# Mixture-of-experts layer of a float32 encoder: four conditional places per expert instead of six, and the two token comparisons nested the other way round

## The chip, the cores and the metric

The kernel runs on one core of a Trainium2 chip. The metric is the device time of one execution in microseconds (us); the figure of a kernel is the median of its runs. Rows of the profile call the engines PE (TensorE, matmuls), PEld (its weight loads), DVE (VectorE), ACT (ScalarE), POOL (GpSimd) and SP (SyncE, which issues most DMAs). An L and a number is a line of the kernel, as printed below.

## The reference, cut to what matters

Two layers of an encoder for 512 tokens of width 1024, all in float32. The change touches only the feed-forward part of the second layer, where each token goes to two of eight experts:

```python
logits = hf @ w_router + b_router            # (512, 8)
top_logit, top_idx = lax.top_k(logits, 2)
gate = softmax(top_logit)
# the rows of each expert are gathered, and for every expert e
y = (silu(x_e @ w1[e]) * (x_e @ w3[e])) @ w2[e]      # w1, w3: 1024 x 1408, w2: 1408 x 1024
# and each token gets the sum of its two rows, times their gates
```

How many tokens an expert gets depends on the data; 1024 picks over eight experts make 128 on average.

## The kernel before

The experts are worked through one after the other. Each expert's weights come as 35 **pieces** of 128 rows, numbered by `SEQ`: 0 to 7 and 8 to 15 are the first two 512-wide thirds of w1 and w3 (`u0`, `u1`), 16 to 19 the rows of w2 for the first third (`d0`), 20 to 27 the last, 384-wide third of w1 and w3 (`u2`), 28 to 31 and 32 to 34 the rest of w2 (`d1`, `d2`). A piece is 512 KB, those of `u2` 384 KB.

A piece is fetched by a DMA of SP (L1289) into one of 18 buffers `raw` (two of them are called `wraw`). Then ACT copies it to a rounded high part `whi` (L1304) and DVE subtracts that to get the low part `wlo` (L1306): this is `cut`, and it runs four pieces ahead of the matmuls in a ring of five pairs. Expert e has two sets of rows:

- **A**, its first 128 tokens: `A(j)` multiplies piece j in three passes (high by high, high by low, low by high) with two matmuls each (L1353); the first pass reads `whi`, the second `wlo`.
- **B**, tokens 129 to 192, if there are any: `B(lo, hi, before)` multiplies pieces lo to hi-1 in one pass straight from `raw` (L1357), for 32 more rows or for 64. It stands inside conditions on `cv[e]`, the number of tokens. Such a spot is called a **place** here. `before` names a third whose result is first transposed by PE into the bank `pub` (`turn`, L1393) and copied by ACT to `gB` (L1398); the `u` pieces of B add up in the same bank `pub`, the `d` pieces in another, `pdb`.

Since B reads `raw`, a buffer is free only when B is through with its piece, or when the place has been passed. So `refill` stands at the end of `B`: it fetches piece n + 18 once B has done piece n. After the place `B(8, 16)` that is pieces 26 to 33, after `B(16, 20)` 34 and the next expert's 0 to 2.

PE, ACT and DVE run in the order of the code (a manual schedule); the order of SP's queue is set by the framework. Every engine meets the conditions; one that skips a place still counts up its semaphore there, and for PE that waits until its own matmuls have ended. SP has work inside a condition only where `yb`, the 64 rows' result, is written out (L1411).

The order of one expert before, with `ahead` true for expert 6 alone:

```python
A(*range(8))
B(0, 8)
A(8, 9, 10, 11); turn(0, 128); A(12, 13, 14, 15)
B(8, 16, 0)
A(16, 17, 18); turn(1, 128); A(19)
B(16, 20, 1)
A(*range(20, 28))
B(20, 28)
A(28); half_T(e + 1, 0); A(29); half_T(e + 1, 1); A(30); turn(2, 128); A(31)
B(28, 35 if ahead else 32, 2)
A(32, 33, 34)
if not ahead: B(32, 35)
```

Behind the last expert `merge` splits the results `pd` (of A) and `pdb` (of B) into high and low parts (L163) and spreads them over the tokens with matmuls (L1436).

Of the kernel before, what the change touches and what calls it, by code (L numbers as in the profile page):

```python
# [25 lines left out]
NK = 8  # L26
# [3 lines left out]
NE = 8  # L30
# [14 lines left out]
def trunk(ctx, tc, I, out, dbg=None):  # L45
# [1053 lines left out]
    def moe(j, l, N, nxt):  # L1099
# [104 lines left out]
        def token_ids(es, b, ps, whole=True, make=True, count=True):  # L1204
            c = slice(b * 128, (b + 1) * 128)
            for e in es:
                oh_e = ohs[(2 * e + b) % 3]
                if make:
                    for t in range(NT):
                        ts(oh_e[:, t, :], iota256[:, c], posm[:, t, e:e + 1], None, op0=OP.is_equal)  # L1210
                for t in range(NT if count else 0):
                    done = mm(ps[:, (b * NE + e) * 2:(b * NE + e) * 2 + 2], oh_e[:, t, :], tk2[:, t, :],
                              start=(t == 0), stop=(t == NT - 1))
            if count:
                tm.append(done)
            if whole:
                return numbers(es, b, ps)

        def numbers(es, b, ps):
            q = slice(es[0], es[-1] + 1)  # L1220
            nc.vector.tensor_reduce(out=tif[:, b, q], in_=ps[:, 16 * b:16 * b + 16].rearrange("p (e c) -> p e c", c=2)[:, q],
                                    axis=AX.X, op=OP.add)
            return nc.vector.tensor_copy(TI[:, b, q], tif[:, b, q])

        def gather(xg, idx, src=hd):
            return nc.gpsimd.indirect_dma_start(out=xg, out_offset=None, in_=src,  # L1226
                                         in_offset=bass.IndirectOffsetOnAxis(ap=idx, axis=0))
# [30 lines left out]
        SEQ = []  # L1258
# [32 lines left out]
        def fetch_any(n, er=None):  # L1291
            if n < NW:
                fetch(n, er, nc.sync if er is None else nc.gpsimd)
            else:
                nc.sync.dma_start(out=raws[n % NRAW].rearrange("p (a b) -> p a b", a=2), in_=tail[n - NW])
# [12 lines left out]
        def rows_T(xg, he, banks):  # L1308
            n = xg.shape[0]
            per = 512 // n  # L1310
            for h in range(NK // per):
                for k in range(per):
                    done = nc.tensor.transpose(banks[h][:, k * n:(k + 1) * n],
                                        xg[:, (per * h + k) * 128:(per * h + k + 1) * 128], ident[0:n, 0:n])
                p3 = banks[h].rearrange("p (k q) -> p k q", k=per)
                if n == 128:
                    split(p3, he[0][:, per * h:per * h + per, :], he[1][:, per * h:per * h + per, :])
                else:
                    act(he, p3, AF.Copy)
            return done  # L1320
# [8 lines left out]
        def quads(m, i):  # L1329
            return m == 32  # L1330
# [33 lines left out]
        def evac(i, m):  # L1364
            fw = FCH[i][1]
            if m == 128:
                src, gated = (tA[1] if i == 2 else tA[i])[:, :fw], tA[i % 2][:, :fw]
                act(src, pa_[2 * (i % 2)][:, :fw], AF.Silu)
                (ordered if i == 2 else partial(tt, op=OP.mult))(out=gated, in0=src, in1=pa_[2 * (i % 2) + 1][:, :fw])
            else:  # L1370
                n, w_ = (64, fw // 2) if quads(m, i) else (m, fw)
                act(tB[i % 2][64:64 + n, :w_], pub[0:n, :w_], AF.Silu)
                f = ordered if i == 2 and m == 64 else partial(tt, op=OP.mult)
                f(out=tB[i % 2][0:n, :w_], in0=tB[i % 2][64:64 + n, :w_], in1=pub[64:64 + n, :w_])
# [38 lines left out]
        def fold(m):  # L1413
            gather((xa, ye)[m % 2], G.slot[:, m % 2, m // 2:m // 2 + 1], yd)

        def add(m):
            t, i = m // 2, m % 2
            stt(X[t], (xa, ye)[i], G.gate[i][:, t:t + 1], X[t], op0=OP.mult, op1=OP.add)
# [21 lines left out]
        def expert(e, he, hb=None, total=NW + len(tail), base=None, er=None):  # L1440
            base = e * NP if base is None else base
            last = er is None and e == NE - 1
            state = {"a": 0, "b": 0, "cut": 0, "got": 0}

            def refill():
                while state["got"] < state["b" if er is None else "a"]:
                    n = base + state["got"] + NRAW
                    if n < total:
                        fetch_any(n, er)
                    state["got"] += 1  # L1450

            def hook(j):
                if e > 0 or er is not None:
                    return
                if j == 6:
                    rows_T(xb, heB[0], (pub,))
                    gather(xb, TI[0:64, 1, 1:2])
                if 3 <= j < 15:
                    i = j - 1
                    token_ids([i // 2 + 1], i % 2, (pd[0], pdb)[i % 2], whole=False, make=False)  # L1460
                if 2 <= j < 14:
                    token_ids([j // 2 + 1], j % 2, None, whole=False, count=False)
                if j == 14:
                    for b in range(2):
                        numbers(range(2, NE), b, (pd[0], pdb)[b])

            def A(*js):
                for j in js:
                    m = j // 2 - 8
                    if last and j % 2 == 0 and 0 <= m < 2 * NT:  # L1470
                        fold(m)
                    piece(base + j, 0, he)
                    hook(j)
                    state["a"] = j + 1
                    n = base + j + AHEAD
                    if n < total:
                        cut(n)
                        if er is None and 0 < e < 4:
                            next(rest, None)
                    if last and j % 2 and 0 < m <= 2 * NT:  # L1480
                        add(m - 1)
                    if SEQ[j][0] == "u" and SEQ[j][2] == NK - 1:
                        evac(SEQ[j][1], 128)
                    if er is not None:
                        refill()

            def B(lo, hi, before=None):
                if er is not None:
                    return

                def rest_of(m):
                    if before is not None:
                        turn(before, m)
                    for j in range(lo, hi):
                        piece(base + j, 1, hb, m)
                    if SEQ[hi - 1][0] == "u":
                        evac(SEQ[hi - 1][1], m)
                    if hi == NP and not last:
                        put(yd[NE * 128 + e * 64:NE * 128 + e * 64 + 64, :], m, nc.sync)

                if last:
                    with tc.If(cv[e] > 128):
                        rest_of(64)
                else:
                    with tc.If(cv[e] > 160) as c:
                        rest_of(64)
                    with c.Else():
                        with tc.If(cv[e] > 128):  # L1508
                            rest_of(32)
                state["b"] = hi  # L1510
                refill()

            A(*range(8))
            B(0, 8)
            A(8, 9, 10, 11)
            turn(0, 128)
            A(12, 13, 14, 15)
            B(8, 16, 0)
            A(16, 17, 18)
            turn(1, 128)  # L1520
            A(19)
            B(16, 20, 1)
            A(*range(20, 28))
            B(20, 28)
            A(28)
            if er is None:
                half_T(e + 1, 0)
            A(29)
            if er is None:
                half_T(e + 1, 1)  # L1530
            A(30)
            turn(2, 128)
            if er is None and e + 1 < NE:
                rows_T(xb, heB[(e + 1) % 2], (pa_[2],))
            A(31)
            ahead = er is None and e == NE - 2
            B(28, 35 if ahead else 32, 2)
            A(32, 33, 34)
            if er is None and not last:
                put(yd[e * 128:(e + 1) * 128, :], 128, nc.sync)  # L1540
            if not ahead:
                B(32, 35)
            if last:
                merge()

# [28 lines left out]
        cv = [nc.values_load(iei[:, e:e + 1], min_val=0, max_val=S) for e in range(NE)]  # L1574
# [351 lines left out]
```

## Time and profile before

| | |
|---|---|
| median of 3 runs | 1956.09 us (1955.92 to 1959.73) |
| profiled execution | 1956.71 us, its span 1955.2 us |
| PE busy | 1903.8 us, 97% of the span |
| DVE, ACT, POOL busy | 1186.8, 908.1, 332.7 us |
| DMA in the whole span | 309.39 MB, mean 158 GB/s |

The profiled execution is one of the program's; the span is what the trace covers. Busy time is summed over stages with different limits, so a change in one stage is read from the rows of that stage: the experts run from about 1388 us to 1890 us of the span. A time in a row of a timeline is the start of a group of like instructions, and the next number is how long the group was busy. Matmuls overlap, so the distance of two starts tells what a matmul takes of PE's time.

### The profile page before, as it was taken

The page shows a single profiled execution, that of the slowest core. Times are in us where ns is not written, and L with a number is a line of the kernel's source. Part 1 is how long each engine was busy: PE and PEld are TensorE (multiplying, and loading weights), DVE is VectorE, ACT ScalarE, POOL GpSimd, SP SyncE. Part 2 cuts the span into 40 slices and gives each one's busy share as a digit, 9 for nine tenths or more (in the row PEclk, how much of TensorE's full clock was granted, in tenths as well). Part 3 has the DMA queues.
Part 4 walks back from the last instruction along what each step waited for, and adds up shares of the span by engine and source line. Part 5 has one row for each costly group of instructions (what it writes and reads, how often), then busy time and mean ns, then how long its engine had stood idle before and what let it go on. Part 6 is the DMA issues. An engine that isn't in the chain of part 4 may idle for free. (4 is left out here: it accounts for less than half of the span.)

```text
span 1955.2 us, 27356 instructions
## 1 busy us (share of the span) xinstructions
PE 1903.8 (97%) x9954; PEld 1511.0 (77%) x9954; DVE 1186.8 (61%) x1859; ACT 908.1 (46%) x1349; POOL 332.7 (17%) x632
## 2 busy tenths in 40 slices
PE   7999999999999999999999999999999999999998
PEld 7787777888888888888787677887678877667666
DVE  5867565754333333345767565745899987666674
ACT  5535434333322222254534435333678876556553
POOL 2058220220000000001048320321100000000021
PEclk9999999999999999999999999999999999999999
DMA  5432223234433333432433232335699997756852
GB/s 168 120 116 87 77 91 128 84 95 168 137 97 94 101 97 97 119 91 62 135 114 98 66 92 85 126 96 212 236 370 368 371 357 272 264 202 251 326 160 99
DMA packets 95141, 309.39 MB, mean 158 GB/s; under 512 B 12609, under 2 KB 15681, under 8 KB 94978
## 3 DMA queue, kind: packets, MB, share of 16 engines
q1 hardware_dynamic: 89554, 290.06, 43.5%
q0 software_dynamic: 5280, 16.91, 2.5%
q8 instruction: 100, 1.64, 0.3%
q14 instruction: 63, 0.52, 0.1%
q10 hardware_dynamic: 144, 0.26, 0.0%
HBM read 283.59 MB, written 23.60 MB: 157 GB/s over the span
## 5 line engine op out<-in xcount | busy, mean ns | idle before, releaser
L137 ACT ACTIVATE whi<-wraw 128x1024 fp32r<-128x1024 f32 (+2 forms) x211 | 217.6, 1034 | 483.7 <-PE a L158 265.1
L139 DVE TENSOR_TENSOR wlo<-wraw,whi 128x1024 fp32r<-128x1024 f32 (+2 forms) x211 | 260.0, 1237 | 265.2 <-ACT whi L137 262.9
L157 PE MATMUL a<-hT_hi,whi 128*128 128x512 f32 (+3 forms) x1056 | 412.3, 391 | 1.4 <-ACT hT_hi L163 0.7
L158 PE MATMUL a<-hT_lo,whi 128*128 128x512 f32 (+3 forms) x1056 | 411.5, 390 | 0.8 <-DVE hT_lo L163 0.7
L159 PE MATMUL a<-hT_hi,wlo 128*128 128x512 f32 (+3 forms) x1056 | 411.6, 390 | 0.6 <-DVE wlo L139 0.6
L1306 DVE TENSOR_TENSOR wlo<-raw,whi 128x1024 fp32r<-128x1024 f32 (+1 forms) x198 | 227.8, 1159 | 45.1 <-ACT whi L1304 31.7
L158 PEld LDWEIGHTS a<-hT_lo,whi 128*128 128x128 f32 (+1 forms) x1056 | 197.1, 187 | 42.9 <-issue 2.8
L159 PEld LDWEIGHTS a<-hT_hi,wlo 128*128 128x128 f32 (+1 forms) x1056 | 197.1, 187 | 42.1 <-issue 3.2
L157 PEld LDWEIGHTS a<-hT_hi,whi 128*128 128x128 f32 (+1 forms) x1056 | 196.7, 187 | 42.5 <-issue 1.6
L1304 ACT ACTIVATE whi<-raw 128x1024 fp32r<-128x1024 f32 (+1 forms) x198 | 198.8, 1009 | 48.1 <-PE a L1353 30.4
L157 PE MATMUL a<-whi,hT_hi 128*128 128x256 f32 (+2 forms) x328 | 110.0, 335 | 1.1 <-ACT hT_hi L163 1.1
L159 PE MATMUL a<-whi,hT_lo 128*128 128x256 f32 (+2 forms) x328 | 109.0, 333 | 0.3
L158 PE MATMUL a<-wlo,hT_hi 128*128 128x256 f32 (+2 forms) x328 | 108.6, 331 | 0.0
L664 POOL TENSOR_TENSOR A<-A,t 128x512 f32<-128x512 f32 x48 | 76.4, 1625 | 179.2 <-DVE t L663 179.2
L1353 PE MATMUL a<-whi,heA_hi 128*128 128x512 f32 (+1 forms) x304 | 91.6, 382 | 4.7 <-PEq L1508 1.8
L1353 PE MATMUL a<-wlo,heA_hi 128*128 128x512 f32 (+1 forms) x304 | 88.7, 373 | 0.0
L1353 PE MATMUL a<-whi,heA_lo 128*128 128x512 f32 (+1 forms) x304 | 88.6, 372 | 0.0
L1353 PEld LDWEIGHTS a<-whi,heA_hi 128*128 128x128 f32 x304 | 54.2, 188 | 22.0 <-issue 8.3
L173 POOL TENSOR_SCALAR rs<-ss 128x1 f32<-128x1 f32 x8 | 2.3, 283 | 393.1 <-ACT sq L1773 392.7
L157 PEld LDWEIGHTS a<-whi,hT_hi 128*128 128x128 f32 x328 | 62.5, 191 | 7.0 <-ACT hT_hi L163 1.6
L159 PEld LDWEIGHTS a<-whi,hT_lo 128*128 128x128 f32 x328 | 62.5, 191 | 5.9 <-DVE hT_lo L163 0.9
L1226 POOL DMA_INDIRECT xa<-hd,TI x8 | 12.4, 1553 | 319.0 <-PE a L1326 310.8
(532 smaller groups left out, 3622.5 us busy)
## 6 DMA issues: line engine op xcount, KB each, us to landing
raw<-in_moe_w13a SPq DMA_DIRECT2D x113, 512.0 KB, 7.5
raw<-in_moe_w SPq DMA_DIRECT2D x74, 512.0 KB, 7.9
wraw<-in_w_gate SPq DMA_DIRECT2D x64, 512.0 KB, 3.6
wraw<-in_ffn_w SPq DMA_DIRECT2D x64, 512.0 KB, 3.6
raw<-in_moe_w13b SPq DMA_DIRECT2D x61, 384.0 KB, 7.2
wraw<-in_w_in_T SPq DMA_DIRECT2D x20, 512.0 KB, 3.3
wraw<-in_w_branch SPq DMA_DIRECT2D x16, 512.0 KB, 3.6
wraw<-in_w_o SPq DMA_DIRECT2D x16, 512.0 KB, 3.6
```

Source lines behind the costliest of these rows:

```text
L137: act(hi[:, :n], raw[:, :n], AF.Copy)
L139: tt(out=lo[:, :n], in0=raw[:, :n], in1=hi[:, :n].bitcast(F), op=OP.subtract)
L157: mm(o, a[0], b[0], start=start, stop=False)
L158: mm(o, a[0], b[1], start=False, stop=False)
L159: mm(o, a[1], b[0], start=False, stop=stop)
L173: gts(out=r[:, :n], in0=ss, scalar1=1.0 / dim, scalar2=EPS, op0=OP.mult, op1=OP.add)
L664: gtt(out=A[m], in0=A[m], in1=g[m], op=OP.add)
L1226: return nc.gpsimd.indirect_dma_start(out=xg, out_offset=None, in_=src, in_offset=bass.IndirectOffsetOnAxis(ap=idx, axis=0))
L1304: act(hi[:, :w], raw[:, :w], AF.Copy)
L1306: return tt(out=lo[:, :w], in0=raw[:, :w], in1=hi[:, :w].bitcast(F), op=OP.subtract)
L1353: mm(dst[x][:, :w_], st[sa][:, k, :], w[:, cs[x]], start=first and q == 0, stop=last and q == 2)
```

## The change

The six places become four. `B(8, 16, 0)` and `B(16, 20, 1)` become `B(8, 20, 0)` behind `A(19)`; the transposes of the second third (`before` = 1) move to `B(20, 28, 1)`; `B(28, 32, 2)` and `B(32, 35)` become `B(28, 35, 2)` behind `A(31)` for every expert. The condition "over 128" is now asked first, with "over 160" inside it. Inside `B`, a third's result is evacuated as soon as its last piece is done, since a place may now go on past it.

```diff
                     for j in range(lo, hi):
                         piece(base + j, 1, hb, m)
-                    if SEQ[hi - 1][0] == "u":
-                        evac(SEQ[hi - 1][1], m)
+                        if SEQ[j][0] == "u" and SEQ[j][2] == NK - 1:
+                            evac(SEQ[j][1], m)
...
                 else:
-                    with tc.If(cv[e] > 160) as c:
-                        rest_of(64)
-                    with c.Else():
-                        with tc.If(cv[e] > 128):
+                    with tc.If(cv[e] > 128):
+                        with tc.If(cv[e] > 160) as c:
+                            rest_of(64)
+                        with c.Else():
                             rest_of(32)
...
             turn(0, 128)
-            A(12, 13, 14, 15)
-            B(8, 16, 0)
-            A(16, 17, 18)
+            A(12, 13, 14, 15, 16, 17, 18)
             turn(1, 128)
             A(19)
-            B(16, 20, 1)
+            B(8, 20, 0)
             A(*range(20, 28))
-            B(20, 28)
+            B(20, 28, 1)
...
-            ahead = er is None and e == NE - 2
-            B(28, 35 if ahead else 32, 2)
+            B(28, 35, 2)
             A(32, 33, 34)
...
-            if not ahead:
-                B(32, 35)
```

On PE, the place behind piece 27 of the first expert (L1505 asks "over 128", L1506 "over 160"; `cst`, `ut` are the transposes' operands, `yh` holds B's rows):

```order
 L1505 COMPARE_AND_BRANCH
+L1506 COMPARE_AND_BRANCH
+L1393 MATMUL b<-cst,ut 128x64 x4
 L1357 MATMUL b<-raw_11228,yh 64x384 x2
 L1357 MATMUL b<-raw_11229,yh 64x384 x2
```

The four transposes now stand ahead of the `u2` matmuls, and both write the bank `pub`.

On SP, the first expert's second place; `wraw` and `raw_11660` to `raw_11665` are the buffers of pieces 8 to 15, into which pieces 26 to 33 are fetched:

```order
 L1505 COMPARE_AND_BRANCH
-L1505 UNCONDITIONAL_BRANCH
-L1508 COMPARE_AND_BRANCH
-L1508 UNCONDITIONAL_BRANCH x2
+L1506 COMPARE_AND_BRANCH
+L1506 UNCONDITIONAL_BRANCH x2
+L1505 UNCONDITIONAL_BRANCH
 L1289 DMA wraw<-in_moe_w13b 128x768 x2
 L1289 DMA raw_11660<-in_moe_w 128x1024
 L1289 DMA raw_11661<-in_moe_w 128x1024
 L1289 DMA raw_11662<-in_moe_w 128x1024
```

The fetches stand in the same order behind SP's second place; but that place now ends behind `A(19)`, and before it ended behind `A(15)`.

On PE, the end of the last expert (its conditions are at L1502 in both kernels; `gB_11680` and the buffers after it are pieces 32 to 34 of B, `Sel` belongs to `merge`):

```order
 L1353 MATMUL b<-wlo,gA_hi 128x512 x2
 L1353 MATMUL b<-whi,gA_lo 128x512 x2
-L1502 COMPARE_AND_BRANCH
-L1357 MATMUL b<-raw_11233,gB_11680 64x512 x2
-L1357 MATMUL b<-wraw,gB_11680 64x512 x4
-L1502 UNCONDITIONAL_BRANCH x2
 L1436 MATMUL a<-heA_hi,Sel 128x512
 L1436 MATMUL a<-heA_lo,Sel 128x512
```

The matmuls of B's last three pieces, which stood between the end of A and `merge`, have gone from there (they stand ahead of `A(32)` now).

## Rows read from the trace of the kernel before

**Rows 1.** The page, part 3: DMA queue, kind: packets, MB, share of 16 engines.

```profile
q8 instruction: 100, 1.64, 0.3%
```

**Rows 2.** Windows: experts without B, and with: busy us, PEclk, DMA share, GB/s.

```profile
1450.00:1600.00 150.00, 147.17 (x704) 120.63 (x703) 137.99 (x184) 121.58 (x138) 8.61 (x6) 1.00 0.97 369
1600.00:1890.00 290.00, 286.52 (x1800) 199.08 (x1798) 194.70 (x201) 166.93 (x208) 16.83 (x12) 1.00 0.69 254
```

**Rows 3.** Waits of PE, 1380 to 1900 us: total us, times, longest.

```profile
PE a L1353 <- PEq L1508: 1.8, 5, 1.1
PE b L1357 <- ACT gB L1398: 1.7, 4, 0.5
```

**Rows 4.** The matmuls of L1357 (B): ns min/median/max, first and last start.

```profile
L1357 PE MATMUL b<-raw,yh x532: 326/379/644, 1608.9 to 1872.9; 128*32 128x256 f32 x76, 128*32 128x192 f32 x42, 128*64 128x512 f32 x39, 128*64 128x384 f32 x21
```

**Rows 5.** PE's timeline, expert 1 (no B): skipped places behind pieces 15, 19, 27.

```profile
1467.76 0.62 PE L1353 MATMUL a<-wlo,heA_hi 128*128 128x512 f32 x2
1468.21 0.61 PE L1353 MATMUL a<-whi,heA_lo 128*128 128x512 f32 x2
1468.97 0.70 PE L1353 MATMUL b<-whi,gA_hi 128*128 128x512 f32 x2
1469.52 0.62 PE L1353 MATMUL b<-wlo,gA_hi 128*128 128x512 f32 x2
...
1475.31 0.59 PE L1353 MATMUL a<-whi,heA_hi 128*128 128x384 f32 x2
...
1484.03 0.70 PE L1353 MATMUL b<-whi,gA_hi 128*128 128x512 f32 x2
```

**Rows 6.** PE's timeline, expert 4 (32 rows in B): two places that are taken.

```profile
1608.40 0.61 PE L1353 MATMUL a<-r_hi,heA_lo 128*128 128x512 f32 x2
1608.95 3.66 PE L1357 MATMUL b<-raw,yh 128*32 128x256 f32 x64
1612.54 0.73 PE L1353 MATMUL a<-whi,heA_hi 128*128 128x512 f32 x2
1613.11 0.62 PE L1353 MATMUL a<-wlo,heA_hi 128*128 128x512 f32 x2
...
1634.81 1.93 PE L1357 MATMUL b<-raw,gB 128*32 128x256 f32 x32
1636.67 0.61 PE L1353 MATMUL a<-whi,heA_hi 128*128 128x384 f32 x2
```

**Rows 7.** Windows of 2 us around the second place of expert 1; columns as before.

```profile
1468.00:1470.00 2.00, 1.85 (x9) 1.24 (x8) 2.00 (x5) 1.72 (x3) 0.00 (x0) 1.00 0.11 25
...
1476.00:1478.00 2.00, 2.00 (x14) 2.00 (x13) 1.76 (x5) 1.36 (x3) 0.00 (x0) 1.00 1.02 410
```

**Rows 8.** SP's timeline: expert 1's piece 28 is issued.

```profile
1469.86 0.37 SPq L1289 DMA_DIRECT2D wraw<-in_moe_w  x1
```

**Rows 9.** DMA issues, 1469.8 to 1470.2 us: KB each, us to landing.

```profile
wraw<-in_moe_w SPq DMA_DIRECT2D x1, 512.0 KB, 6.4
```

**Rows 10.** Timelines of ACT and DVE: the cut of one 512 KB piece.

```profile
1467.50 1.06 ACT L1304 ACTIVATE whi<-raw 128x1024 fp32r<-128x1024 f32 x1 [0.30 <-DVE c L1611]
...
1468.61 1.22 DVE L1306 TENSOR_TENSOR wlo<-raw,whi 128x1024 fp32r<-128x1024 f32 x1
```

**Rows 11.** Timelines of PE, ACT and DVE at the end of the last expert.

```profile
1887.05 0.61 PE L1353 MATMUL b<-whi,gA_lo 128*128 128x512 f32 x2
1888.50 1.89 PE L1357 MATMUL b<-wraw,gB 128*64 128x512 f32 x8
1890.32 0.50 PE L1436 MATMUL a<-heA_hi,Sel 128*128 128x512 f32 x1
1892.15 0.40 PE L1436 MATMUL a<-heA_hi,Sel 128*128 128x512 f32 x1
...
1887.48 1.08 ACT L163 ACTIVATE heA_hi<-b 128x512 fp32r<-128x512 f32 x2 [6.08 <-PE b L1353]
...
1888.10 1.29 DVE L163 TENSOR_TENSOR heA_lo<-b,heA_hi 128x512 fp32r<-128x512 f32 x2 [2.44 <-ACT heA_hi L163]
```

## The prediction

> **What bounds the kernel now.** I read the windows first. [...] Without B the DMA engines are busy for 0.97 of the time at 369 GB/s; with B for 0.69. The 704 matmuls of the first window are 2.97 experts (35 pieces x 6, and 27 transposes, make 237 each), so an expert without B lasts 50.5 us, and its DMAs 0.97 x 50.5 = 49.0 us. Below that PE can't bring it, whatever it saves.
>
> The first B matmul starts at 1608.9 us [rows 4]. Experts 0 to 3, the 210 us and more before that, therefore skip every place; 4 to 7 take them, 4 and 6 with 32 rows, 5 and 7 with 64.
>
> Then the places themselves. Two pairs of matmuls stand 0.45 us apart. Across the skipped place behind piece 15 the distance is 0.76, and the pair behind it takes 0.55 [rows 5]: PE empties itself, and fills again. A skipped place costs 0.31 + 0.10, some 0.40 us. Of the 24 such places the list of waits counts only what is above its threshold, 1.8 us [rows 3].
>
> **The change, part by part.**
>
> Skipped places: two fewer in each of experts 0 to 3, 8 x 0.40 = -3.2 us. That the outer comparison is now "over 128" saves a branch on the way past; I cost it at nothing, since the next matmul waits for PE's own last matmul, and the branches lie under that wait. [...]
>
> Taken places: the step into B costs 0.55 - 0.45 = 0.10, the pair behind it 0.57 - 0.45 = 0.12 [rows 6]. 64 matmuls of B and the step out take 3.59 us, 32 take 1.86: so 2 x 1.86 - 3.59 = 0.13 of it is the step out. That is 0.35 us a place. Experts 4, 5 and 7 lose two places, expert 6 one, since it had five: 7 x 0.35 = -2.45 us. In expert 5 (64 rows; expert 7 has one comparison only, as before) a second comparison is now passed at each place; I cost that at nothing, since PE's matmuls of A, already queued, cover the branch.
>
> The transposes of the second third: before, they stood ahead of `d0`, which adds up in `pdb`. Now they stand ahead of `u2`, which adds up in `pub`, the bank that they themselves write. The first `u2` matmul must wait until ACT has copied `pub` to `gB`. That wait is there already at the place behind piece 15, four times, 1.7 us [rows 3]; it stays there and comes a second time: +1.7 us.
>
> The moved fetches: pieces 26 to 33 are issued when the second place is over, and that is now A(20)'s start, not A(16)'s: 1475.31 - 1468.97 = 6.3 us later, less the 0.4 of the place that is gone [rows 5]. Nothing covers this well in experts 0 to 3. At that very moment the DMA engines have run dry: share 0.11 from 1468 to 1470, and 1.02 some microseconds later [rows 7]. What is late next is piece 28, the first of 512 KB. It is issued at 1469.86, 0.89 us behind the place's end, and lands after 6.4 us [rows 8, 9], 7.3 us behind the end. ACT's and DVE's parts of its cut take from 1467.50 to 1469.83, 2.33 us [rows 10], with some 0.1 us of handing over; PE needs the low part only in its second pair, 0.45 us after the start. So A(28) can start 7.3 + 2.0 = 9.3 us behind the end of the second place, and PE comes to it 1484.03 - 1475.31 = 8.7 us behind [rows 5]. The stall is 0.6 us an expert, 2.3 us for four, if the queue is dry each time. It may not be: where the pieces of one expert come 5.9 us later, so do those behind them, and the queue that ran dry about 1468 would then run dry about 1474, just ahead of the new place. Then there is no fresh start and no stall. Bounds 0 and 2.3 us; I take the middle, +1.2 us. In experts 4 to 7, B's own matmuls lie between (3.6 us at the first place alone, rows 6), and with a DMA share of 0.69 I cost the delay at nothing there.
>
> The fetches behind `yb` on SP: SP waits inside the last place for B's result. That place now ends ahead of A(32) to A(34), so the wait ends earlier by three pieces (3 x 3 x 0.45 = 4.1 us), while some fetches that stood ahead of it now stand behind. I cost it at nothing; the cover is the next expert's first pieces, which are in their buffers by then.
>
> The end: B's last three pieces covered the splitting of `pd` before `merge`. The last pair of A starts at 1887.05, its second matmul 0.23 later, at 1887.28. ACT and DVE split two banks from 1887.48 to 1889.39; a third bank, `pdb`, would take half of 1.29 us more on DVE, to about 1890.0, and the fifth matmul of `merge` comes 0.25 later, 3.0 us behind the last matmul of A. Before, it started at 1892.15, and the last of B at 1888.50 + 1.89 - 0.64 (the longest of L1357, rows 4) = 1889.75: 2.4 us [rows 11]. So +0.6 us.
>
> Sum: -3.2 - 2.45 + 1.7 + 1.2 + 0.6 = **-2.15 us**, all of it in the experts. The profiled execution took 1956.71 us and would take 1954.6; the median of the runs is 0.6 us lower, so the forecast in its terms is **1953.9 us**. That is 0.11% less; a difference of under 0.2% (3.9 us) is about what a measurement of this kernel can't tell from no change.
>
> **The rivals.**
>
> *No new stall.* The queue never runs dry at the new place, and `merge` starts as it did: -3.2 - 2.45 + 1.7 = -3.95, 1952.1 us. For it: the DMA cycle of 49.0 us is still under the new 50.5 - 0.8 = 49.7. Against it: only by 0.7 us.
>
> *The switches cost nothing worth saving.* If a merged place drains as long as two did (skipped 0.2, taken 0.1 saved each), the sum is -1.6 - 0.7 + 1.7 + 1.2 + 0.6 = +1.2, 1957.3 us. For it: the rows show the cost of a place, not that of leaving one out. Against it: two drains can hardly lie in one.
>
> *The weights come too late* (slower). The place is experts 0 to 3: the delayed pieces don't catch up, since the DMA engines have 0.7 us an expert to spare, and each piece of the next expert meets PE late as well. Without stalls the sum is -3.35; it is 3.9 us slower from stalls of 7.3 us in all, 1.8 an expert, that is from a landing of piece 28 at 8.5 us behind the place instead of 7.3. With 2.5 us an expert: -3.35 + 10 = +6.7, 1962.8 us. For it: 0.97. Against it: the buffers hold 18 pieces, half an expert, and the next expert's pieces wait in them.
>
> *Longer jumps miss the code.* The place `B(8, 20)` holds half as many more instructions as the longest before, and so does a jump past it; if a skip had to wait for code, that is 1 fetch each: the queue q8 spends 0.3% of 16 x 1955 us on 100 packets, 0.9 us each [rows 1]. Two longer jumps in each of four experts: 8 x 0.9 = +7.2, with the sum +5.1, 1961.1 us. For it: nothing but the size. Against it: 24 skipped places with 1.8 us of counted waits in all [rows 3], so a jump of the present length does not wait for 0.9 us. [...]
>
> **How the numbers follow.** Forecast 0.50; no new stall 0.20; nothing to save 0.17; weights too late 0.08; code 0.05. The range takes in the first three, with 0.5 us for the unlike runs: 1951.6 to 1957.6. Faster by over 0.2% (under 1952.2): half of the second case and 0.05 of the first, 0.15. Slower (over 1960.0): most of the last two, 0.10. Within: 0.75.
>
> **What would show it.** Right: in experts 0 to 3, four distances of about 0.76 between pairs instead of six; one new wait of PE of a few tenths at A(28), ended by a cut that DMA `raw` or `wraw` held up; eight waits for `gB` with 3.4 us; the DMA share in such an expert near 0.98, its dry moment moved to A(20); a wait ahead of L1436 of about 0.6 us more. Wrong: waits of PE for cuts of other pieces than 28, above all of the next expert's; skipped places with over 0.5 us; a pair behind a place that is not 0.10 slower.

## The result, and the profile after

The changed kernel takes **1969.04 us** (median of 7 runs, 1965.72 to 1974.36), the kernel before in the same measurement 1956.61 us (7 runs, 1955.92 to 1959.73): a ratio of 1.0063, interval 1.0053 to 1.0073. It is 0.63% slower, where a loss of over 0.2% had a chance of 0.10. The span of the profiled execution grew from 1955.2 to 1965.8 us, by less than the median; the two longest of the seven runs (1972.45 and 1974.36 us) have the lowest mean granted clock, 0.995, against 0.997 in the profiled one.

First, where. These are the first matmuls of A(0) of expert 0 and of expert 4 in PE's timeline, before and after:

```profile
1387.62 0.62 PE L1353 MATMUL a<-whi,heA_hi 128*128 128x512 f32 x2
1597.88 0.71 PE L1353 MATMUL a<-whi,heA_hi 128*128 128x512 f32 x2
```

```profile
1387.07 0.62 PE L1353 MATMUL a<-whi,heA_hi 128*128 128x512 f32 x2
1602.12 0.62 PE L1353 MATMUL a<-whi,heA_hi 128*128 128x512 f32 x2
```

Experts 0 to 3, where B is skipped, last 215.05 us and lasted 210.26: +4.8, where the sum had -3.2 + 1.2 = -2.0. From expert 4 to the end of the span it is 363.7 us and was 357.3: +6.4, where the sum had -2.45 + 1.7 + 0.6 = -0.15. The stages ahead of the experts give the missing -0.6.

Second, what PE waits for. The list of its waits after the change, 1380 to 1900 us (us in total, times, longest); of before it is [rows 3]:

```profile
PE b L1357 <- ACT gB L1398: 5.3, 7, 2.7
PE a L1313 <- DVE heA_lo L163: 4.9, 4, 1.4
PE b L1357 <- issue: 2.4, 1, 2.4
...
PE b L1353 <- ACT gA_hi L163: 0.5, 1, 0.5
...
PE a L1353 <- ACT whi L1304: 0.4, 1, 0.4
```

The wait for `gB` was 1.7 us; together with the 2.4 us put down to "issue", at the same spot in expert 4, it is now 7.7. The wait of L1313 for `heA_lo` is new. L1313 is the transposing of the next expert's B rows, which stands between A(30) and A(31) in every expert but the last and reuses the bank that `half_T(e + 1, 0)` filled; it can't begin until DVE has read that bank (L163).

Third, why these are late. ACT's waits for weight pieces, 1450 to 1600 us, after the change; before, the list has no wait for a DMA at all:

```profile
ACT whi L1304 <- DMA raw<-in_moe_w: 4.5, 10, 1.8
ACT whi L1304 <- DMA wraw<-in_moe_w: 2.3, 3, 2.0
ACT whi L1304 <- DMA raw<-in_moe_w13b: 2.3, 3, 0.9
```

And the windows after the change: experts without B, and two windows around the end of the new second place of expert 1 (columns as in [rows 2]):

```profile
1450.00:1600.00 150.00, 143.66 (x684) 117.90 (x683) 133.37 (x181) 116.43 (x134) 5.67 (x6) 0.99 0.92 359
1474.00:1475.00 1.00, 0.99 (x5) 0.46 (x3) 0.70 (x2) 0.96 (x2) 0.00 (x0) 1.00 0.00 0
1475.00:1477.00 2.00, 1.86 (x11) 1.89 (x12) 1.78 (x3) 1.37 (x2) 0.00 (x0) 1.00 0.42 104
```

The DMA engines stand still until the place ends, so the queue does run dry at the new place, and their share falls from 0.97 to 0.92. Piece 26 is issued at 1475.11 us, as A(20) starts at 1475.14. The chain from there to PE, in the timelines of ACT, DVE and PE of expert 1:

```profile
1478.20 0.85 ACT L1304 ACTIVATE whi<-raw 128x768 fp32r<-128x768 f32 x1 [0.87 <-DMA raw<-in_moe_w13b]
1479.88 0.85 ACT L1304 ACTIVATE r_hi<-wraw 128x768 fp32r<-128x768 f32 x1 [0.84 <-DMA wraw<-in_moe_w13b]
...
1482.92 1.23 DVE L1306 TENSOR_TENSOR wlo<-wraw,whi 128x1024 fp32r<-128x1024 f32 x1 [1.12 <-ACT whi L1304]
...
1488.76 1.22 DVE L1306 TENSOR_TENSOR r_lo<-raw,r_hi 128x1024 fp32r<-128x1024 f32 x1 [0.21 <-ACT r_hi L1304]
...
1489.97 0.68 DVE L163 TENSOR_TENSOR heA_lo<-a,heA_hi 128x512 fp32r<-128x512 f32 x1
...
1490.71 0.71 PE L1313 MATMUL a<-cst,xb 64*128 64x64 f32 x8 [1.23 <-DVE heA_lo L163]
```

The same rows of DVE before, the cut of piece 28 and the reading of the bank:

```profile
1480.85 1.23 DVE L1306 TENSOR_TENSOR wlo<-wraw,whi 128x1024 fp32r<-128x1024 f32 x1 [0.22 <-ACT whi L1304]
...
1487.84 0.69 DVE L163 TENSOR_TENSOR heA_lo<-a,heA_hi 128x512 fp32r<-128x512 f32 x1
```

DVE read the bank from 1487.84 to 1488.53 before, and PE came to it at 1489.57: 1.0 us to spare. Now it reads it 2.1 us later, though PE is a little earlier, and PE waits for 1.23 us. The delay is there when DVE cuts piece 28 (1482.92 against 1480.85), and from there to the bank the only idle time listed for DVE is the 0.21 us above, so it doesn't shrink. No matmul of A waits for a piece here. What waits stands behind the pieces in the order of ACT and DVE. (The 0.4 us of the list, where A does wait for a cut, are at A(13) of expert 1, at 1464.73 us; ACT had waited 0.88 us for a landing some cuts earlier.)

In experts 4 to 7 it is ACT's copy to `gB`. PE and ACT in expert 6, at the place behind piece 27:

```profile
1796.45 0.33 PE L1393 MATMUL b<-cst,ut 64*128 64x64 f32 x2
1799.47 4.49 PE L1357 MATMUL b<-raw,yh 128*32 128x192 f32 x64 [2.68 <-ACT gB L1398]
...
1796.38 1.06 ACT L1304 ACTIVATE whi<-raw 128x1024 fp32r<-128x1024 f32 x1 [0.19 <-PE a L1353]
1797.81 1.06 ACT L1304 ACTIVATE whi<-raw 128x1024 fp32r<-128x1024 f32 x1 [0.37 <-DMA raw<-in_moe_w]
1798.77 0.47 ACT L1368 ACTIVATE ut<-a 128x384 f32<-128x384 f32 x1
1799.14 0.27 ACT L1398 ACTIVATE gB<-b 128x128 f32<-128x128 f32 x1
```

The transposes are done at 1796.8 (1796.45 + 0.33). ACT copies them at 1799.14, since the cuts of pieces 28 to 31 and the evacuation of A stand ahead of the copy, and those pieces land late. The 64 matmuls behind the wait then take 4.49 us; the same 64 took 2.81 before:

```profile
1791.50 2.81 PE L1357 MATMUL b<-raw,yh 128*32 128x192 f32 x64
```

The windows of the wait and of these matmuls show the granted clock (behind the five busy times): 1.00 while PE is idle, then 0.56:

```profile
1796.80:1799.40 2.60, 0.00 (x0) 0.00 (x0) 2.37 (x3) 2.23 (x4) 0.00 (x0) 1.00 1.03 422
1799.40:1802.40 3.00, 2.93 (x40) 2.03 (x44) 1.34 (x3) 0.01 (x1) 0.00 (x0) 0.56 1.02 419
```

### The profile page after: what moved, and what is told of

The parts are those of the page before. It is cut to its first block, busy times and chain, and to the rows that moved or that the text cites. A ratio compares the mean times of both kernels' runs of the same rounds, so it can differ in the third digit from the quotient of the medians.

```text
span 1965.8 us, 27098 instructions
## 1 busy us (share of the span) xinstructions
PE 1904.0 (97%) x9954; PEld 1515.0 (77%) x9954; DVE 1185.2 (60%) x1859; ACT 905.3 (46%) x1349; POOL 326.3 (17%) x632
## 5 line engine op out<-in xcount | busy, mean ns | idle before, releaser
L158 PEld LDWEIGHTS a<-wlo,hT_hi 128*128 128x128 f32 x328 | 62.7, 191 | 4.7
```

What stands on the lines that cost most here:

```text
L158: mm(o, a[0], b[1], start=False, stop=False)
```

## The experiments

Two causes are to be told apart: the **late fetches** (pieces 26 to 33 issued behind A(19) instead of A(15)), and the **moved transposes** (ahead of `u2`, with ACT's copy behind four cuts). The ends of the experts and the nesting of the comparisons are checked as well. Ratios are to the kernel before, run on the same chip.

**Parts of the change.** `e1_nest`: only the comparisons are nested the other way.

```diff
-                    with tc.If(cv[e] > 160) as c:
-                        rest_of(64)
-                    with c.Else():
-                        with tc.If(cv[e] > 128):
+                    with tc.If(cv[e] > 128):
+                        with tc.If(cv[e] > 160) as c:
+                            rest_of(64)
+                        with c.Else():
```

> Six places as before, only the comparisons are nested the other way round. Fetch theory (the loss of the change comes from pieces 26 to 33, which are issued about 6 us later): no difference, 1956.6 us within 2 us. Nesting theory (the order of the comparisons costs or saves something at each place): 24 skipped places with one comparison fewer, or 64-row places with one more, by up to 0.1 us each, so 1954 or 1959 us, and skipped places whose distance is no longer 0.76 us.

Measured: 0.9998 (0.9989 to 1.0007). The order of the comparisons is worth nothing that can be measured.

`e2_mid`: the middle alone, with the evacuation inside `B` that it needs.

```diff
-            A(12, 13, 14, 15)
-            B(8, 16, 0)
-            A(16, 17, 18)
+            A(12, 13, 14, 15, 16, 17, 18)
             turn(1, 128)
             A(19)
-            B(16, 20, 1)
+            B(8, 20, 0)
             A(*range(20, 28))
-            B(20, 28)
+            B(20, 28, 1)
```

> Only the middle is changed: one place for pieces 8 to 19 behind A(19), and the transposes of the second third ahead of u2. The end of an expert and the comparisons are as before. Fetch theory: the whole loss is here, 1968 to 1971 us, with PE's waits for DVE's heA_lo in experts 0 to 3 (about 4.9 us in all) and for gB in 4 to 7 (over 5 us). Rival (the loss is at the merged last place): under 1960 us.

Measured: 1.0052 (1.0038 to 1.0065), waits for `heA_lo` 5.8 us, for `gB` and "issue" 5.6. The loss is here.

`e3_end`: the end alone.

```diff
-            ahead = er is None and e == NE - 2
-            B(28, 35 if ahead else 32, 2)
+            B(28, 35, 2)
...
-            if not ahead:
-                B(32, 35)
```

> Only the end of an expert is changed: one place for pieces 28 to 34. Fetch theory: four skipped places fewer by 0.31 us, two taken ones by 0.25, and 0.8 us more ahead of the merge of the last expert, so 1955.7 us, no difference that can be measured. Rival (the merged last place is what costs): over 1962 us.

Measured: 0.9996 (0.9987 to 1.0005), as expected.

**Late fetches alone, two misses.** `e4_late`: six places, and only the refill moved.

```diff
-                state["b"] = hi
-                refill()
+                if hi != 16:
+                    state["b"] = hi
+                    refill()
```

> Six places, transposes, and comparisons as before; only the fetches of pieces 26 to 33 are moved from the place behind A(15) to the one behind A(19). Fetch theory: experts 0 to 3 lose 1.5 to 1.9 us each by PE's wait for DVE's heA_lo and its followers, some 6.5 us in all, and 4 to 7 lose nothing since their transposes are where they were: 1963 us. Rival (the moved transposes make the whole loss, and the late fetches are hidden): 1956.6 us within 1 us.

Measured: 1.0002 (0.9993 to 1.0011). It tells nothing about either theory. SP's rows stand in the same order as before, so piece 26 still went out when the place behind A(15) was over (in expert 1 at 1471.34 us, as A(16) starts at 1471.37): here the fetch went out when the place behind the last reader of its buffer was over, not at the spot where the refill is written.

`e9_hold`: eight readers behind A(19), to keep those buffers.

```diff
+            if er is None:
+                for j in range(8, 16):
+                    raw = raws[(base + j) % NRAW]
+                    mm(pdb[0:32, 0:8], raw[:, 0:32], raw[:, 32:40], start=True, stop=True)
             B(16, 20, 1)
```

> Six places, transposes and comparisons as before. Behind A(19), eight added matmuls of 8 columns read the buffers of pieces 8 to 15 once more into a bank that the next d0 overwrites, so that those buffers come free only then, and pieces 26 to 33 are fetched then (the output stays the same). The added matmuls take 0.5 us an expert, 4 us. Late fetches as the cause: PE also waits for DVE's heA_lo in experts 0 to 3 as in the changed kernel, 1.2 to 1.5 us each, 6 us in all, and 10 us more than before. Rival (it is the merged place as such, or what else moved with it): no such wait, and 4 us more than before.

Measured: 1.0304 (1.0290 to 1.0319). A miss again: the refill was still written ahead of the readers, so they read pieces 26 to 33, and PE waited 33.2 us for these to land.

**Taking the causes out one by one.** `e5_tmove`: six places and their fetches as before, the transposes moved.

```diff
-            B(16, 20, 1)
+            B(16, 20)
             A(*range(20, 28))
-            B(20, 28)
+            B(20, 28, 1)
```

> Six places and their fetches as before; only the transposes of the second third of B move from ahead of d0 to ahead of u2. Theory of two causes (late fetches, and ACT's copy to gB that stands behind four cuts): the pieces are in time here, so PE's wait for gB there is 0.9 us in each of experts 4 to 7, as it was in 5 and 7 of the changed kernel, and 3.7 us more than before in all; experts 0 to 3 are unchanged. Rival (the moved transposes alone make the waits of 2.7 us and more): 10 us more than before.

Measured: 1.0009 (1.0000 to 1.0018). The waits of PE:

```profile
PE b L1357 <- ACT gB L1398: 3.0, 7, 0.5
```

With 0.4 us put down to "issue" that is 3.4 us, 1.7 more than before and less than half of the 3.7 expected: with pieces in time, the moved transposes cost just what the prediction gave them. The other 4.3 us of the changed kernel's 7.7 come only with late fetches.

`e6_tin`: the changed kernel with the transposes at the end of the second place.

```diff
                             evac(SEQ[j][1], m)
+                    if lo == 8:
+                        turn(1, m)
...
-            B(20, 28, 1)
+            B(20, 28)
```

> The changed kernel, but the transposes of the second third stand at the end of the place for pieces 8 to 19, behind its d0 matmuls. Two causes: PE's waits for gB ahead of u2 go (9.3 us in the changed kernel), the waits for heA_lo in experts 0 to 3 stay: 2 to 3 us more than before. Rival (what waits for gB would wait for the late pieces anyway, a few matmuls later): 8 us more than before or more.

Measured: 1.0017 (1.0008 to 1.0026). The waits for `gB` are back at those of before, those for `heA_lo` stay:

```profile
PE a L1313 <- DVE heA_lo L163: 5.2, 4, 1.7
...
PE b L1357 <- ACT gB L1398: 1.7, 4, 0.5
```

`e7_early`: the changed kernel with the second place behind A(15).

```diff
-            A(12, 13, 14, 15, 16, 17, 18)
-            turn(1, 128)
-            A(19)
+            A(12, 13, 14, 15)
             B(8, 20, 0)
+            A(16, 17, 18)
+            turn(1, 128)
+            A(19)
```

> The changed kernel with its second place moved up: pieces 8 to 19 of B behind A(15) instead of A(19), so that pieces 26 to 37 are fetched at once when A(15) is over. Two causes: no wait for heA_lo in experts 0 to 3, and 0.9 us for gB in each of 4 to 7: 0.5 us less than before. Rival (it is the size of a place or the number of pieces that a place holds, not its moment, that delays): as slow as the changed kernel, 10 us more than before.

Measured: 1.0000 (0.9991 to 1.0009). There is no wait for `heA_lo`; `gB` as in `e5_tmove`. The same merged place with earlier fetches brings no stall of that kind, so it isn't its size. Most of what the places save is lost again: to `gB`, ahead of the merge, and to 2.9 us in which PE waits for its sequencer behind the new second place (L1505, four times; before, the list has 0.6 us of that kind for these matmuls).

`e8_early_tin`: both edits.

> Both: the second place behind A(15), and the transposes of the second third at its end. Two causes: neither wait is left; twelve places saved at 0.3 us skipped and 0.5 us taken, 0.8 us lost ahead of the merge: 4 us less than before. Rival (a skipped place saves nothing once fetches are on time): no difference.

Measured: 0.9990 (0.9981 to 0.9999), about half of what was expected. (The expectation counts twelve places; in all 15 go.) Neither wait is left, but the one at the second place stays:

```profile
PE b L1353 <- PEq L1507: 3.4, 4, 1.7
```

The skipped place behind A(15) took 1.09 us of PE's idle time in expert 1 and 1.72 in expert 3; PE's own sequencer is named, no weight piece.

**Where the place stands.** The kernel of `e8_early_tin`, transposes at the end of the place, with the place behind A(14), A(16), A(17) and A(18). For A(17) the edit of `e7_early` becomes:

```diff
-            A(12, 13, 14, 15, 16, 17, 18)
+            A(12, 13, 14, 15, 16, 17)
+            B(8, 20, 0)
+            A(18)
             turn(1, 128)
             A(19)
-            B(8, 20, 0)
```

Behind A(14), `e10_at14`:

> As the kernel with the second place behind A(15) and the transposes at its end, but the place behind A(14). In that kernel PE waited 0.9 and 1.6 us at this place in experts 1 and 3, with a packet of the instruction queue in those microseconds. [...] Rival (PE waits there for a weight piece that has not landed): longer here, over 1.6 us an expert, since the place asks for piece 19 earlier.

Measured: 1.0562 (1.0547 to 1.0576), and of no use: there the buffer of piece 19 is refilled with piece 37 before it is cut, so A works with another piece in its place, and ACT waits for that piece to land (41.2 us in two waits from 1450 to 1600 us) with everything that stands behind it.

Behind A(16), `e11_at16`:

> The same with the place behind A(16): pieces 26 to 37 are fetched 1.4 us later than behind A(15). Before, DVE had read heA's bank 1.0 us ahead of PE's next use of it; so late fetches should cost 0 to 0.4 us in each of experts 0 to 3. 3 to 4.6 us less than before without a wait for code, 1 to 2.5 us less with it.

Measured: 0.9978 (0.9968 to 0.9989), no wait for `heA_lo`; PE waits 2.3 us for its sequencer at the place (three times, longest 1.6), which is the wait that the expectation puts down to code.

Behind A(17), `e12_at17`:

> The same with the place behind A(17): fetches 2.8 us later than behind A(15). If the loss grows with the delay beyond a margin of 1.0 us, PE's wait for heA_lo is there again, 0.3 to 1.2 us in each of experts 0 to 3 (it was 0.9 to 1.8 behind A(19)): 1 to 3 us less than before, less a wait for code if one falls here. Rival (the loss comes only when the queue has run dry): no wait for heA_lo, as behind A(15).

Measured: 0.9977 (0.9968 to 0.9986), no wait for `heA_lo` either, 1.4 us at the place. That is 5.2 us less than before (1953.45 against 1958.66), where a margin of 1.0 us would have left 1 to 3. The rival's outcome came, but not for its reason, that the loss comes only when the queue has run dry: the DMA engines stand all but still ahead of this place too, without a loss:

```profile
1470.00:1471.00 1.00, 0.85 (x5) 0.42 (x3) 1.00 (x3) 0.49 (x2) 0.00 (x0) 1.00 0.02 6
```

Behind A(18), `e14_at18`:

> Place for pieces 8 to 19 behind A(18), transposes at its end. Behind A(17) PE never waited for heA_lo, behind A(19) 1.3 us an expert. If the delay costs nothing until a margin of some 4 us is used up and then grows one for one: 0 to 0.6 us an expert here, 3 to 5 us less than before. If it is the moment ahead of the transposes of A that decides: as behind A(19), 3 us more than before.

Measured: 0.9980 (0.9971 to 0.9989). PE has no wait for `heA_lo` at L1313 here, though ACT already waits for landings (11 waits on pieces of `u0` and `u1` alone, 4.8 us from 1450 to 1600 us). In expert 1, piece 26 is issued at 1471.80 us, 1.9 us ahead of A(20) (1473.66); behind A(19) it is issued as A(20) starts, and PE waits 1.1 to 1.4 us an expert. Behind A(18) the late pieces are paid out of the margin, behind A(19) the margin is used up.

**Late fetches alone, done rightly.** `e13_hold2`: the readers of `e9_hold`, and the refill left out at the place behind A(15) as in `e4_late`, so that it stands behind the readers.

> Six places as before. The fetches of pieces 26 to 33 now wait: behind A(19), eight added matmuls of 8 columns read the buffers of pieces 8 to 15 once more (into a bank that the next d0 overwrites; the output stays the same), and the refill stands behind them. The added matmuls take 0.5 to 0.9 us an expert, 4 to 7 us. Late fetches as the cause: PE's wait for DVE's heA_lo appears in experts 0 to 3 with six places too, 0.9 to 1.8 us each, so 8 to 14 us more than before; none in 4 to 7. Rival (it takes the merged place): no wait for heA_lo, 4 to 7 us more than before.

Measured: 1.0057 (1.0044 to 1.0071), 1970.02 against 1958.41 us. PE's waits, with six places:

```profile
PE a L1313 <- DVE heA_lo L163: 3.6, 3, 1.4
```

A(0) of expert 0 starts at 1388.66 us and that of expert 4 at 1607.66: 219.0 us, 8.7 more than before. The readers take 0.6 us an expert (A(20) begins 2.39 us behind A(19), before 1.79), so 6.3 us of it are late fetches. From A(0) of expert 4 to the end of the span it is 1967.7 - 1607.66 = 360.0 us, 2.7 more than before, of which the readers take 2.4: there late fetches alone cost next to nothing. `gB` is at 1.7 us as before. The rival, that it takes the merged place, falls.

**A version that beats both.** `e15_best`: the place behind A(17), transposes at its end (the edit inside `B` is that of `e6_tin`), and in the last expert the two places at the end as before.

```diff
-            A(12, 13, 14, 15, 16, 17, 18)
+            A(12, 13, 14, 15, 16, 17)
+            B(8, 20, 0)
+            A(18)
             turn(1, 128)
             A(19)
-            B(8, 20, 0)
             A(*range(20, 28))
-            B(20, 28, 1)
+            B(20, 28)
...
-            B(28, 35, 2)
+            B(28, 32 if last else 35, 2)
...
             if last:
+                B(32, 35)
                 merge()
```

> Place behind A(17), transposes at its end, and in the last expert alone the two places at the end as before, so that B's last three pieces cover the splitting ahead of the merge again. Merge theory: 0.85 us less than the kernel with the place behind A(17), that is 6 us less than before. Rival (the second place at the end costs as much as it covers): no difference between the two.

Measured: 0.9972 (0.9961 to 0.9983), 1953.32 against 1958.41 us. PE's list has no `heA_lo` of L1313, and `gB` at 1.7 us. The windows show the experts without B near the busy time and DMA share of before [rows 2]:

```profile
1450.00:1600.00 150.00, 147.92 (x714) 122.97 (x713) 138.94 (x187) 122.63 (x139) 8.06 (x6) 1.00 0.96 374
```

Against the kernel behind A(17) the two intervals overlap. In the traces, from A(0) of expert 7 to the end of the span it is 1951.7 - 1808.65 = 143.05 us against 1951.5 - 1807.53 = 143.97: 0.9 us, as the merge theory had it.

## Why the prediction was wrong

**Skipped and taken places: right.** In `e15_best`, which has no new stall, A(0) of expert 0 starts at 1389.75 us and that of expert 4 at 1596.79: 207.04 us, 3.2 less than before, with eight skipped places less. That is the -3.2 of the sum, at 0.40 each: with PE busy for 147.17 of 150 us before [rows 2] and for 147.92 here, what the places took of its time comes off the time. `e3_end` has the same price by itself: from A(0) of expert 0 to that of expert 4 it is 1598.34 - 1389.67 = 208.67 us, 1.6 less for four skipped places. In `e15_best`, from A(0) of expert 4 to that of expert 7, at 1808.65, it takes 211.86 us, and took 1811.69 - 1597.88 = 213.81: 1.95 less for five taken places (two each in 4 and 5, one in 6), 0.39 each instead of 0.35. The rival by which a merged place drains as long as two did is out.

**The moved fetches: this step failed.** The prediction asked when PE needs piece 28, found a stall of 0 to 0.6 us an expert at A(28), and took +1.2 us in all. The mechanism at its start was right: the queue runs dry at the new place (share 0.00 in the window above), and pieces 26 onward land late. PE's need was about right too: the third pair of A(28) starts 1.07, 1.00, 1.25 and 1.22 us behind the first in experts 0 to 3, before 1.00 to 1.01, so A(28) loses 0.5 us in all. What was not followed is what stands behind the cuts on ACT and DVE. Both take it in the order of the code, and DVE is busy for 138 of 150 us [rows 2]; in expert 1 it is 2.1 us late at the cut of piece 28 and still 2.1 us late at `heA_lo`, and ACT's `gA_hi` comes late with it.

With the places saving 3.2 us as above, experts 0 to 3 lost 4.8 + 3.2 = 8.0 us to new stalls, not 1.2. Of these, 4.9 + 0.5 + 0.4 = 5.8 us stand in the list. Some 1.4 us are no wait: in expert 2, behind the wait at L1313, the granted clock was 0.50 from 1543.80 to 1547.10 us (last section). Most of the rest is A(28). Two kernels with the clock at 1.00 in these experts agree: `e13_hold2` has 6.3 us from late fetches alone, and `e6_tin` takes 1602.64 - 1389.42 = 213.22 us for experts 0 to 3, 6.2 more than `e15_best`. The 1.0 us between DVE and PE at L1313 was there to be read in the trace of before. It isn't the whole margin of a fetch: behind A(18) fetches come later than before and PE still doesn't wait.

"In experts 4 to 7 [...] I cost the delay at nothing there" holds for late fetches alone (`e13_hold2`), but not for this change: the cover that was named, B's matmuls and a DMA share of 0.69, covers A. It does not cover ACT, which has four of the late pieces to cut before it copies `gB`, and it is the moved transposes that make PE wait for that copy.

**The moved transposes: the term was right by itself, and wrong beside the late fetches.** +1.7 us was predicted and `e5_tmove` shows 1.7, in the eight waits of 3.4 us that the prediction named; in the changed kernel the waits grew by 6.0 us. To that comes 4.49 - 2.81 = 1.7 us, where the granted clock was 0.50 from 1799.80 to 1803.10 us. With the 2.45 us saved at taken places and the merge, experts 4 to 7 make -2.45 + 6.0 + 1.7 + 0.8 = +6.05, against +6.4 measured.

**The end: right, a little small.** Behind the last matmul of A (its pair starts at 1899.36, and the second 0.23 later) the fifth matmul of L1436 starts at 1902.79, 3.2 us later, where 3.0 was predicted; so +0.8 instead of +0.6. (A slip that changes nothing: by its own words the range ends at 1957.3 + 0.5 = 1957.8, not at 1957.6.)

**The rivals.** The slower one, "the weights come too late", came true in its size (2.0 us an expert, where it asked for 1.8 to be slower by 0.2%), but not in its place: it had each piece of the next expert meet PE late, and the list has 0.4 us of that, at A(13) of expert 1. It had a chance of 0.08 because the buffers were thought to cover PE, and ACT and DVE were not asked. "Longer jumps miss the code" is not what slowed the changed kernel: its list has 1.1 us for PE's sequencer behind skipped places, before it had 2.4 (L1508; [rows 3] shows 1.8 of them, and one wait, at the very first place, was 1.1). But with the place behind A(15) to A(18), PE did wait there, up to 1.7 us. What these waits were for, no run here shows: in `e8_early_tin` the instruction queue has one packet from 1468 to 1470 us, about the wait of 1.09 us, and one from 1567 to 1571, about that of 1.72; but in the kernel before it has one from 1468.0 to 1468.5 and one from 1475 to 1476 us too, within 1 us of two skipped places for which the list has no wait.

## What to carry to other kernels

When a fetch moves, follow it to every engine that touches the data, and on each ask what stands behind it in that engine's order and who waits for that; the margin of the matmul that uses the data is not the margin of the kernel. Two edits that are cheap alone can be dear together, where one makes an engine late and the other puts a wait behind it: in experts 4 to 7 late fetches alone cost some 0.3 us and the moved transposes alone 1.7, and together they made PE wait 6.0 us more and run 1.7 us longer in the 3.3 us with the granted clock at 0.50. Merging two conditional places is worth 0.4 us each here, but the merged place should stand where the buffers come free no later than the margins allow (up to A(18) here), not where the last of its pieces is used.

## What was not expected of the hardware

Twice in the experts the granted clock fell to 0.50 behind a wait of PE. In expert 6 PE had been idle for 2.68 us; the clock was 0.50 from 1799.80 to 1803.10 us, and 64 matmuls took 1.7 us longer (rows above). In expert 2 it had waited for only 1.42 us, at L1313:

```profile
1542.80 0.71 PE L1313 MATMUL a<-cst,xb 64*128 64x64 f32 x8 [1.42 <-DVE heA_lo L163]
1543.43 0.99 PE L1353 MATMUL b<-whi,gA_hi 128*128 128x512 f32 x2
...
1547.22 0.63 PE L1353 MATMUL b<-r_lo,gA_hi 128*128 128x512 f32 x2
```

```profile
1541.00:1543.40 2.40, 0.98 (x12) 0.71 (x10) 2.40 (x3) 2.40 (x5) 0.00 (x0) 1.00 1.02 418
1543.80:1547.10 3.30, 3.15 (x8) 2.07 (x7) 3.30 (x5) 2.30 (x3) 0.88 (x1) 0.50 1.03 418
```

From the first pair of A(31) to the second of A(32) that is 3.79 us; before, it was 2.34:

```profile
1540.97 0.73 PE L1353 MATMUL b<-whi,gA_hi 128*128 128x512 f32 x2
...
1543.31 0.63 PE L1353 MATMUL b<-r_lo,gA_hi 128*128 128x512 f32 x2
```

In expert 1 a like wait of 1.23 us left the clock at 1.00, and in expert 4 PE stood idle for 2.41 us at the place where expert 6 lost its clock, and kept it:

```profile
1650.00:1655.00 5.00, 3.54 (x67) 3.06 (x68) 2.92 (x5) 1.99 (x5) 0.00 (x0) 1.00 1.04 420
```

So the length of the single idle stretch did not tell here whether the clock would fall, and two stalls cost more than the wait that the list shows: 1.7 us more in expert 6, 3.79 - 2.34 = 1.45 us in expert 2.
